# A hybrid decoder layer: the scan's decay by select and biased exponentials, the gated norm's scale at the output projection, q/k roots in batches of four

## The chip, the cores and the metric

The kernel runs on one core of a Trainium2 chip. The metric is the device time of one execution in microseconds (us); lower is better. Engines are named as in the profile: PE (TensorE, matmuls), PEld (its weight loads), DVE (VectorE), ACT (ScalarE), POOL (GpSimd), SP (the queue that issues the DMAs).

## What is computed

One layer of a decoder over 2048 tokens of width 1024, float32. One input projection feeds three branches, whose outputs are joined (512 + 1024 + 512 columns) and mapped back by one output projection:

```python
u = rms_norm(h, norm_g)
q, k, v, z_att, f_raw, z_ssd, xbc, dt_raw, x_lru, z_lru = split(u @ w_in)
y_att = fox_attention(rms_norm(q), rms_norm(k), v, log_sigmoid(f_raw + b)) * silu(z_att)
y_ssd = ssd_mixer(xbc, dt_raw, z_ssd, ...)      # 16 heads x 64, 2 groups, state 128, chunks of 128
y_lru = rglru_mixer(x_lru, ...) * silu(z_lru)
out = h + concat(y_att, y_ssd, y_lru) @ w_out
```

Inside `ssd_mixer`, for each chunk of 128 tokens and each of the 2 groups of 8 heads:

```python
seg  = a_cs[l] - a_cs[s]                  # running sums of the log decay, per head
lmat = exp(where(l >= s, seg, -inf))      # decay, 0 above the diagonal
y    = (C B^T * lmat) @ (x dt)  +  (C @ state) * exp(a_cs)  +  x * d_skip
state = state * exp(total) + B^T @ (x dt * exp(a_cs[-1] - a_cs))
gated = rms_norm(y * silu(z), over the group's 512 columns) * norm_g
```

## The kernel before

**Precision.** A float32 matrix product is made of float32r matmuls: each operand is split into a high part (a cast) and a low part (operand minus high part), and three products are summed in PSUM. So a product over 1024 channels is 8 x 3 matmuls of 128 rows.

**Stages.** (1) x is loaded, normalised, transposed and split (L195-292). (2) `weights` (L172) brings groups of 256 columns of `w_in` to SBUF, eight tiles each, ACT casting the high part (L186) and DVE or POOL making the low part (L187); the tiles turn over in a pool of `NSL` = 11 high and 11 low slots (L161). There are 22 such groups. First come the columns of x, B, C with convolution and silu (L379-413), then the first v/z group, then the linear recurrent branch (L484-576), then z of the state-space branch (L579-591), with `gates` (L416) ahead of its second group. (3) The scan: `ssd_unit` (L608) for 16 chunks x 2 groups, and written after it the projections of q, k, v and z in four column groups (L737-766, `group_vz` L328). On the chip these two run interleaved. (4) Attention (L787-895): per head and 256 queries, scores, exponentials, transposes of the probabilities, product with v. Between its steps a filler is fed in: the first sweep of the output projection (L929-976), over the rows of `w_out` that need no attention (state-space group 1 and the recurrent branch). (5) The second sweep, over state-space group 0 and attention.

**Order.** Each engine runs its queue in order. The program is written in the order above; the Tile framework orders each engine's queue when the program is built and inserts the semaphores. `fill` (L987) advances the filler by 256 ticks over 288 steps of attention; one tick is the three matmuls of one row tile of `w_out`.

**The scan's unit.** Five loads from DRAM (x, z, B, B and C transposed). PE makes the scores `cb` (L623), DVE masks them with `tri` into `cbm` (L625). Per half of the heads (4 heads), the running sums are loaded as rows to all partitions (`ab`, L637), POOL subtracts the column's own sum (L638), DVE clamps to at most 0 (L640), ACT takes the exponential of 512 columns at once (L641), POOL multiplies by `cbm` (L642), and PE multiplies each head's tile with x dt (L645). DVE adds the skip term (L649) and the part from the carried state (L652-656), and multiplies by the gate (L657). ACT squares and sums (L661), DVE takes the inverse root in twelve small instructions (L662, `rsqrt` L110, three Newton steps), ACT scales y (L664). For the next state, ACT and POOL split B and the scaled x (L599), and PE makes three float32r products into `pn` (L604-606). The state is decayed by POOL and added by DVE (L680-682). `store` transposes y and writes it to DRAM. The five PSUM tiles of a unit (`cb`, `py`, `po`, `pn`, `pty`) share a pool of three banks.

**q and k.** For each of 8 pairs of token tiles: projection (`proj_tok2`), copy and squares by ACT, sums by DVE (L748), `rsqrt` on 8 columns, scaling (L753), four transposes, then high and low parts (L762-764) and stores. The tile `qk` has two buffers, and `group_vz` takes its `vs` tile from the same ones.

**Output projection.** Per token tile and 512 output columns, 8 row tiles x 3 matmuls sum into one PSUM bank (L971-973); DVE adds the residual (L974). `parts` names the two kinds of four row tiles. The first sweep has one PSUM bank, the second five.

Of the kernel before, what the change touches and what calls it, by code (L numbers as in the profile page):

```python
# [8 lines left out]
F32 = mybir.dt.float32  # L9
F32R = mybir.dt.float32r  # L10
# [3 lines left out]
ALU = mybir.AluOpType  # L14
# [4 lines left out]
P = 128  # L19
# [8 lines left out]
NSL = 11  # L28
# [14 lines left out]
def hybrid_block(ctx, tc, x, norm_g, w_in, q_norm_g, k_norm_g, forget_b, ssd_conv_w, ssd_conv_b,  # L43
# [45 lines left out]
    tri = ctile("tri", [P, P])          # 1 where column >= partition  # L89
# [12 lines left out]
    acs = ctile("acs", [P, NT, 16])  # L102
    eacs = ctile("eacs", [P, NT, 16])
    dec = ctile("dec", [P, NT, 16])
    etot = ctile("etot", [P, NT, 16])
    lsp = ctile("lsp", [P, 4])
    nlsp = ctile("nlsp", [P, 4])

    # y = v ** -0.5 by Newton's method from a first guess on the bits of v
# [10 lines left out]
    # y = -(v * scale + EPS) ** -0.5 of one column: a root, then one of Newton's steps  # L120
# [9 lines left out]
    # y = log(1 + exp(xin))  # L130
# [23 lines left out]
    # ======================= input projection =======================  # L154
# [7 lines left out]
    # the two parts of u, transposed: [512 tokens][channel tile]  # L162
# [9 lines left out]
    def weights(cols, rawp=wrp, eng=V):  # L172
        """cols: list of (first column, width). Returns the two parts of the float32 weights."""
# [20 lines left out]
    with tpool(name="p0", bufs=2) as p0, tpool(name="p01", bufs=1) as p01, \  # L194
# [71 lines left out]
        for tb in range(4):  # L266
# [12 lines left out]
            if tb == 0:  # L279
# [4 lines left out]
                # halve what goes into silu(y) = (1 + tanh(y / 2)) * (y / 2); 1/8 of the logits; signs  # L284
# [43 lines left out]
    def group_vz(pool, p):  # L328
# [4 lines left out]
        for t2 in range(8):  # L333
            vs = pool.tile([P, 2, 2, P], F32R, name=f"vs{p}_{t2}", tag="qk")
# [80 lines left out]
    rtx.close()  # L415
    def gates(g1):  # L416
# [20 lines left out]
        acs2 = acs.rearrange("p a b -> p (a b)")  # L437
# [42 lines left out]
    group_vz(g0, 0)  # L480
    g0x.close()

# [115 lines left out]
    # the two parts of a tile  # L598
    def split(src, h, l):  # L599
        A.copy(h, src)  # L600
        G.tensor_tensor(l, src, h.bitcast(F32), op=ALU.subtract)

    def mm3(ps, st, mv):
        T.matmul(ps, st[0], mv[0], start=True, stop=False)  # L604
        T.matmul(ps, st[0], mv[1], start=False, stop=False)
        T.matmul(ps, st[1], mv[0], start=False, stop=True)

    def ssd_unit(c, g):  # L608
# [15 lines left out]
        cbm = s1.tile([P, P], F32, name=f"cbm{u}", tag="cbm")  # L624
        V.tensor_tensor(cbm, pc[:, 0:P], tri, op=ALU.mult)  # L625
# [7 lines left out]
        for q in range(2):  # L633
# [4 lines left out]
            G.tensor_tensor(ab, ab, acs[:, c, qs].unsqueeze(2).broadcast_to([P, 4, P]),  # L638
                            op=ALU.subtract)
            V.tensor_scalar(ab, ab, 0.0, None, op0=ALU.min)  # L640
            A.activation(ab, ab, AF.Exp)  # L641
            G.tensor_tensor(ab, ab, cbm.unsqueeze(1).broadcast_to([P, 4, P]), op=ALU.mult)  # L642
# [16 lines left out]
        ss = s2.tile([P, 1], F32, name=f"ss{u}", tag="ss")  # L659
        rs = s2.tile([P, 1], F32, name=f"rs{u}", tag="rs")  # L660
# [76 lines left out]
    with tpool(name="ap", bufs=2) as pool, tpool(name="ap1", bufs=1) as ap1:  # L737
        for p in range(4):
# [28 lines left out]
            if p > 0:  # L767
                group_vz(pool, p)
# [269 lines left out]
```

## Time and profile before

| | |
|---|---|
| runs of the kernel | 2180.85, 2184.38, 2186.16 us; median 2184.38 |
| span of the profiled execution | 2186.6 us, 2.2 us above that median |
| mean granted TensorE clock | 0.973 of full |

The profile's own execution is timed by its span. "Busy" is the time in which an engine ran instructions; PE's matmuls overlap, so the mean length of one is longer than the step from one to the next. "Idle before ... <- X" is the time that an engine stood before instructions of a group, and what ended it. A group's line gives line of code, engine, operation, output <- inputs, shapes, count | busy us, mean ns of one | idle before it.

### The profile page before, as it was taken

The numbers are of one execution on the slowest core, as the hardware profiler recorded it, in microseconds if no ns is written. First come the engines' busy times: TensorE is split into PE (matmuls) and PEld (weight loads), VectorE is DVE, ScalarE is ACT, GpSimd is POOL, SyncE is SP. The second block draws the span as 40 slices with busy tenths as digits, with TensorE's granted clock in tenths as the row PEclk, the third lists the DMA queues.
The fourth block names the chain that finished last, engine by engine and source line by source line (L and its number), as shares of the span: only waits on it lengthen the run. The fifth ranks groups of instructions, "written<-read, shape, count | busy, mean of one in ns | idle before, by whom it ended". The sixth has DMA issues, their size and how long they took to land. (4 is left out here: it accounts for less than half of the span.)

```text
span 2186.6 us, 36465 instructions
## 1 busy us (share of the span) xinstructions
PE 2038.9 (93%) x12515; PEld 1795.1 (82%) x12515; DVE 1439.2 (66%) x3342; ACT 958.2 (44%) x1885; POOL 697.2 (32%) x874
## 2 busy tenths in 40 slices
PE   7999999999999997888878889899999999998999
PEld 6788889877799987777778778788888888887887
DVE  6655563688772179986998795667777777775211
ACT  7444442566621133332334332555565556554110
POOL 0000011555400046656666651133332323222110
PEclk9999999999999999899899999899999999999999
DMA  5122243111123244454445546753554355224443
GB/s 192 49 58 68 76 114 104 30 40 40 39 82 94 69 119 138 132 155 127 127 121 169 142 122 176 210 141 105 145 151 118 103 144 152 76 67 149 155 136 110
DMA packets 277818, 248.44 MB, mean 114 GB/s; under 512 B 58724, under 2 KB 225152, under 8 KB 275584
## 3 DMA queue, kind: packets, MB, share of 16 engines
q1 hardware_dynamic: 277472, 246.07, 39.0%
q8 instruction: 99, 1.62, 0.3%
q14 instruction: 87, 0.71, 0.1%
q0 software_dynamic: 160, 0.03, 0.1%
HBM read 159.83 MB, written 86.18 MB: 113 GB/s over the span
## 5 line engine op out<-in xcount | busy, mean ns | idle before, releaser
L874 ACT CAST ph<-T 128x512 fp32r<-128x512 f32 (+2 forms) x352 | 162.8, 489 | 159.9 <-PE T L867 115.1
L875 DVE TENSOR_TENSOR pl<-T,ph 128x512 fp32r<-128x512 f32 (+2 forms) x352 | 191.3, 565 | 60.6 <-ACT ph L874 57.2
L971 PE MATMUL po<-woh,mh 128*128 128x512 f32 x512 | 214.6, 419 | 1.9 <-ACT mh L954 1.2
L973 PE MATMUL po<-woh,ml 128*128 128x512 f32 x512 | 201.5, 395 | 0.0
L972 PE MATMUL po<-wol,mh 128*128 128x512 f32 x512 | 200.3, 391 | 0.0
L867 PE MATMUL T<-ident,L 128*128 128x128 f32 x1088 | 171.7, 278 | 9.0 <-ACT L L818 7.5
L818 ACT ACTIVATE L<-L,mx 128x1920 f32<-128x1920 f32 (+15 forms) x128 | 154.5, 1207 | 57.1 <-DVE mx L817 53.4
L373 DVE SCALAR_TENSOR_TENSOR accx<-rtx,cv,accx 128x512 f32<-128x512 f32 x144 | 104.5, 753 | 87.1 <-ACT accx L370 77.1
L322 PE MATMUL pxx<-uh,wh 128*128 128x512 f32 x384 | 153.2, 402 | 4.5 <-ACT rtx L365 3.3
L853 PE MATMUL O<-ph,vv 128*128 128x256 f32 x576 | 153.2, 287 | 2.7 <-ACT ph L874 2.6
L323 PE MATMUL pxx<-ul,wh 128*128 128x512 f32 x384 | 154.0, 402 | 0.0
L314 PE MATMUL pqk<-wh,ul 128*128 128x256 f32 x512 | 153.5, 300 | 0.0
L313 PE MATMUL pqk<-wl,uh 128*128 128x256 f32 x512 | 152.6, 298 | 0.5 <-DVE wl L187 0.5
L312 PE MATMUL pqk<-wh,uh 128*128 128x256 f32 x512 | 152.4, 298 | 0.5 <-ACT wh L186 0.5
L324 PE MATMUL pxx<-uh,wl 128*128 128x512 f32 x384 | 152.6, 399 | 0.0
L854 PE MATMUL O<-pl,vv 128*128 128x256 f32 x576 | 150.9, 288 | 0.4 <-DVE pl L875 0.3
L313 PE MATMUL pzs<-wl,uh 128*128 128x256 f32 x512 | 145.5, 285 | 3.0 <-POOL wl L187 3.0
L312 PE MATMUL pzs<-wh,uh 128*128 128x256 f32 x512 | 145.4, 285 | 0.5 <-ACT wh L186 0.5
L314 PE MATMUL pzs<-wh,ul 128*128 128x256 f32 x512 | 144.4, 283 | 0.0
L867 PEld LDWEIGHTS T<-ident,L 128*128 128x128 f32 x1088 | 127.9, 142 | 19.9 <-ACT L L818 12.0
L807 POOL TENSOR_SCALAR_AFFINE_SELECT cm<-cb 128x384 f32<-128x384 f32 (+3 forms) x128 | 58.8, 460 | 256.6 <-DVE mx L814 210.4
L812 PE MATMUL S<-kh,qh 128*128 128x512 f32 (+2 forms) x320 | 129.3, 405 | 10.7 <-DVE mx L814 7.4
(321 smaller groups left out, 5983.5 us busy)
## 6 DMA issues: line engine op xcount, KB each, us to landing
ab<-acs_d SPq DMA_DIRECT2D x64, 256.0 KB
wr<-in_w_in_dram SPq DMA_DIRECT2D x192, 64.0 KB
wr<-in_w_in_dram SPq DMA_DIRECT2D x80, 128.0 KB
xt<-in_x_dram SPq DMA_DIRECT2D x16, 512.0 KB
xs_d<-stx SPq DMA_DIRECT2D x32, 256.0 KB
v_d<-vs SPq DMA_DIRECT2D x32, 256.0 KB
zs_d<-zs SPq DMA_DIRECT2D x32, 256.0 KB
xs<-xs_d SPq DMA_DIRECT2D x32, 256.0 KB
```

Source lines behind the costliest of these rows:

```text
L312: T.matmul(ps[:, i, :], h[k][:, sl], wh[k], start=(k == 0), stop=False)
L313: T.matmul(ps[:, i, :], h[k][:, sl], wl[k], start=False, stop=False)
L314: T.matmul(ps[:, i, :], l[k][:, sl], wh[k], start=False, stop=(k == KD - 1))
L322: T.matmul(ps, wh[k][:, ms], uh[tb][k], start=(k == 0), stop=False)
L323: T.matmul(ps, wh[k][:, ms], ul[tb][k], start=False, stop=False)
L818: A.activation(lt[:, 0:n], lt[:, 0:n], AF.Exp, bias=mx, accum_out=sm[:, i:i + 1])
L867: ins = T.transpose(pt[:, jj, i * P:(i + 1) * P], L[i][:, kt * P:(kt + 1) * P], ident)
L874: A.copy(ph[:, ja, ca], pt[:, ja, ca])
L875: V.tensor_tensor(pl[:, ja, ca], pt[:, ja, ca], ph[:, ja, ca].bitcast(F32), op=ALU.subtract)
L971: T.matmul(ps, mh[:, j, :], h[:, cs], start=(j == 0), stop=False)
L972: T.matmul(ps, mh[:, j, :], l[:, cs], start=False, stop=False)
L973: T.matmul(ps, ml[:, j, :], h[:, cs], start=False, stop=(j == 7))
```

## The change

Seven edits. `NSL` goes from 11 to 9. In the scan: POOL selects the loaded rows (NEG where the row's token is earlier than the column's), ACT takes four exponentials of 128 columns, each with the head's negated sum as bias, and DVE multiplies with the scores straight from PSUM; the subtraction, the clamp and the masked scores go. The gated norm's sum of squares is kept in `rsn`, the inverse roots of all 32 units are taken at once after the scan, and y is stored unscaled. The next state's product is one float32 matmul without a split. In the output projection, where the scale is now applied, the pieces are 256 columns wide: the two kinds of rows sum into two halves of one bank, and DVE evicts each half by itself, one of them with the scale; the filler advances 512 ticks over the 288 steps. The q/k roots are taken for four pairs of token tiles at once (`NQ` = 4), with five buffers (`QB` = 5) for `qk` and `vs`. The tables `nacs`, `eacs`, `dec` stand in a pool that ends with the scan.

```diff
-NSL = 11
+NSL = 9
+NQ = 4
+QB = 5
...
+    nacs, eacs, dec = (sg.tile([P, NT, 16], F32, name=nm) for nm in ("nacs", "eacs", "dec"))
...
+        V.tensor_scalar(nacs.rearrange("p a b -> p (a b)"), pa[:, 0:256], -1.0, None,
+                        op0=ALU.mult)
...
-        V.tensor_tensor(cbm, pc[:, 0:P], tri, op=ALU.mult)
...
-            G.tensor_tensor(ab, ab, acs[:, c, qs].unsqueeze(2).broadcast_to([P, 4, P]),
-                            op=ALU.subtract)
-            V.tensor_scalar(ab, ab, 0.0, None, op0=ALU.min)
-            A.activation(ab, ab, AF.Exp)
-            G.tensor_tensor(ab, ab, cbm.unsqueeze(1).broadcast_to([P, 4, P]), op=ALU.mult)
+            G.affine_select(out=ab, in_=ab, pattern=[[0, 4], [1, P]], compare_op=ALU.is_ge,
+                            fill=NEG, base=0, channel_multiplier=-1)
+            for e in range(4):
+                i = g * 8 + q * 4 + e
+                A.activation(ab[:, e, :], ab[:, e, :], AF.Exp, bias=nacs[:, c, i:i + 1])
+            V.tensor_tensor(ab, ab, pc[:, 0:P].unsqueeze(1).broadcast_to([P, 4, P]),
+                            op=ALU.mult)
...
-        A.activation(sq, y2, AF.Square, accum_out=ss)
-        V.tensor_scalar(ss, ss, 1.0 / 512.0, 4.0 * EPS, op0=ALU.mult, op1=ALU.add)
-        rsqrt(s2, rs, ss, 1, f"rg{u}")
-        A.activation(y2, y2, AF.Copy, scale=rs)
+        A.activation(sq, y2, AF.Square, accum_out=rsn[:, c, g:g + 1])
...
-            split(bm, bh, bl)
...
-            split(x2, xh, xl)
-            mm3(pn, (bh, bl), (xh, xl))
+            T.matmul(pn, bm, xe.rearrange("p h d -> p (h d)"), start=True, stop=True)
...
+    V.tensor_scalar(rs2, rs2, 1.0 / 512.0, 4.0 * EPS, op0=ALU.mult, op1=ALU.add)
+    V.tensor_copy(rsv, rs2)
+    rsqrt(s2, rs2, rsv, NT * 2, "rg")
...
+            for th in range(8 // NQ):
...
+                for i in range(NQ):
...
+                    V.tensor_reduce(ss[:, i, :], sq.rearrange("p i (h d) -> p (i h) d", d=64),
+                                    axis=AX.X, op=ALU.add)
...
+                rsqrt(ap1, r2_, s2_, NQ * 8, f"rk{p}{th}")
+                for i, qk in enumerate(qks):
...
-            for n in range(2):
-                cs = slice(n * 512, n * 512 + 512)
+            for n in range(4):
+                cs = slice(n * 256, n * 256 + 256)
...
-                ps = psP.tile([P, 512], F32, name=f"po{t}_{n}_{ks[0]}", tag="P")
+                ps = psP.tile([P, 2, 256], F32, name=f"po{t}_{n}_{ks[0]}", tag="P")
...
-                    T.matmul(ps, mh[:, j, :], h[:, cs], start=(j == 0), stop=False)
+                    o = ps[:, j // 4, :]
+                    T.matmul(o, mh[:, j, :], h[:, cs], start=(j == 0), stop=False,
+                             skip_group_check=True)
...
-                V.tensor_tensor(xr, xr, ps, op=ALU.add)
+                for j, (kind, _) in enumerate(parts):
+                    if kind in (0, 1):
+                        V.scalar_tensor_tensor(xc, ps[:, j, :], rsn[:, t, kind:kind + 1], xc,
+                                               op0=ALU.mult, op1=ALU.add)
+                    else:
+                        V.tensor_tensor(xc, xc, ps[:, j, :], op=ALU.add)
...
-        want = count[0] * 256 // 288
-        if want > count[1]:
-            count[1] = want
+        want = count[0] * 512 // 288
+        while want > count[1]:
+            count[1] += 1
```

More of the change, by code (lines that the diff above doesn't have):

```diff
@@ L333, in group_vz @@
         for t2 in range(8):
-            vs = pool.tile([P, 2, 2, P], F32R, name=f"vs{p}_{t2}", tag="qk")
+            vs = vpool.tile([P, 2, 2, P], F32R, name=f"vs{p}_{t2}", tag="qk")
             zt = pool.tile([P, 2, P], F32, name=f"zt{p}_{t2}", tag="zt")
@@ L436, in gates @@
         V.tensor_tensor(adt, dt, alg.unsqueeze(1).broadcast_to([P, NT, 16]), op=ALU.mult)
-        acs2 = acs.rearrange("p a b -> p (a b)")
+        acs2 = g1.tile([P, 256], F32, name="acs")
         pa = psY.tile([P, 512], F32, name="pacs", tag="Y")
@@ L735, in load_q @@
         heads[h][3:] = [qh, ql]
[L737 removed]
+    with tpool(name="ap", bufs=2) as pool, tpool(name="ap1", bufs=1) as ap1, \
+            tpool(name="qkp", bufs=QB) as qkp:
         for p in range(4):
             w = weights([(C_Q + p * P, P), (C_K + p * P, P)])
[L740 to L766 removed]
@@ new lines, in hybrid_block @@
+            for th in range(8 // NQ):
+                ss = pool.tile([P, NQ, 8], F32, name=f"sqk{p}_{th}", tag="sqk")
+                rs = pool.tile([P, NQ, 8], F32, name=f"rqk{p}_{th}", tag="rqk")
+                qks = []
+                for i in range(NQ):
+                    t2 = th * NQ + i
+                    qk = qkp.tile([P, 2, 256], F32, name=f"qk{p}_{t2}", tag="qk")
+                    qks.append(qk)
+                    ps = proj_tok2(w, t2, f"pqk{p}_{t2}")
+                    A.copy(qk, ps)
+                    sq = ap1.tile([P, 2, 256], F32, name=f"sq{p}_{t2}", tag="sqq")
+                    A.activation(sq, ps, AF.Square)
+                    V.tensor_reduce(ss[:, i, :], sq.rearrange("p i (h d) -> p (i h) d", d=64),
+                                    axis=AX.X, op=ALU.add)
+                s2_, r2_ = (z.rearrange("p a b -> p (a b)") for z in (ss, rs))
+                V.tensor_scalar(s2_, s2_, 1.0 / 64.0, EPS, op0=ALU.mult, op1=ALU.add)
+                rsqrt(ap1, r2_, s2_, NQ * 8, f"rk{p}{th}")
+                for i, qk in enumerate(qks):
+                    t2 = th * NQ + i
+                    qv = qk.rearrange("p i (h d) -> p (i h) d", d=64)
+                    V.tensor_tensor(qv, qv, rs[:, i, :].unsqueeze(2).broadcast_to([P, 8, 64]),
+                                    op=ALU.mult)
+                    pt = pst.tile([P, 2, 256], F32, name=f"ptq{p}_{t2}", tag="pt")
+                    for j in range(2):
+                        for i2 in range(2):
+                            T.transpose(pt[:, j, i2 * P:(i2 + 1) * P],
+                                        qk[:, i2, j * P:(j + 1) * P], ident)
+                    ts = slice(t2 * 256, (t2 + 1) * 256)
+                    for j, (wn, gn) in enumerate((("q", "qg"), ("k", "kg"))):
+                        sh = pool.tile([P, 256], F32R, name=f"sth{p}_{t2}_{j}", tag="sth")
+                        sl = pool.tile([P, 256], F32R, name=f"stl{p}_{t2}_{j}", tag="stl")
+                        A.activation(sh, pt[:, j, :], AF.Copy, scale=c1(gn))
+                        V.scalar_tensor_tensor(sl, pt[:, j, :], c1(gn), sh.bitcast(F32),
+                                               op0=ALU.mult, op1=ALU.subtract)
+                        dma(qk_d[wn, "h", p][:, ts], sh.bitcast(F32))
+                        dma(qk_d[wn, "l", p][:, ts], sl.bitcast(F32))
@@ L767, in hybrid_block @@
             if p > 0:
-                group_vz(pool, p)
+                group_vz(pool, qkp, p)
             if p == 2:
```

70 lines of the change are left out of this document (18 added, 52 removed).

## The prediction

> **What bounds the kernel now.** I read the page's shares first, then the busy time of each engine by stage, then what PE waits for inside the worst stage, then the groups of instructions.
>
> ```profile
> span 2186.6 us, 36465 instructions
> ...
> PE 2038.9 (93%) x12515; PEld 1795.1 (82%) x12515; DVE 1439.2 (66%) x3342; ACT 958.2 (44%) x1885; POOL 697.2 (32%) x874
> ...
> PE   7999999999999997888878889899999999998999
> ...
> DVE  6655563688772179986998795667777777775211
> ```
>
> PE is busy 93% of the span, but the slices say that it is not everywhere the limit: about slices 14 to 24 PE stands at 8 tenths or less while DVE stands at 9. That is where the scan of the state-space branch and the q, k, v projections run together. The busy time by stretches (PE, PEld, DVE, ACT, POOL, then the granted clock) gives the size:
>
> ```profile
> 601.30:765.30 164.00, 164.00 (x1382) 163.90 (x1381) 62.30 (x146) 32.48 (x65) 9.73 (x12) 1.00 0.27 81
> 765.30:1366.60 601.30, 504.24 (x3616) 466.50 (x3616) 499.35 (x1241) 214.13 (x475) 338.18 (x308) 0.93 0.49 139
> 1421.30:1967.90 546.60, 538.06 (x3488) 477.27 (x3487) 406.42 (x1165) 318.68 (x640) 163.25 (x319) 1.00 0.44 120
> ```
>
> The first row is pure projection: PE without a gap at full clock. The third is attention with the first output sweep: PE 98%. The middle one is the scan stage: 601.3 us, PE busy 504.2, so 97.1 us idle, and the granted clock is 0.93, so about 601.3 x 0.07 = 42 us of the rest is lost to half-rate time. At full clock the same PE work is 504.2 x 0.93 = 469 us. DVE is busy 499 us there, 83%. What PE waited for inside this stage (total us, times, longest):
>
> ```profile
> PE ptq L757 <- DVE qk L753: 30.3, 15, 5.8
> PE py L645 <- POOL ab L642: 18.8, 16, 1.9
> PE pn L605 <- POOL xel L601: 14.9, 11, 3.0
> PE pty L689 <- DVE yo L654: 7.8, 7, 2.4
> PE pn L604 <- ACT bh L600: 7.6, 8, 1.8
> ```
>
> Five rows carry 79.4 of the 97.1 us, and each waits at the end of a chain over DVE, POOL or ACT which the change cuts. How the gaps reach the clock shows at two of them (start, length, the idle time ahead in brackets) and the 2 us stretch that follows:
>
> ```profile
> 918.73 1.10 PE L645 MATMUL py<-xd,ab 128*128 128x64 f32 x8 [1.76 <-POOL ab L642]
> 923.37 0.66 PE L757 MATMUL ptq<-ident,qk 128*128 128x128 f32 x4 [2.62 <-DVE qk L753]
> 924.00:926.00 2.00, 2.00 (x14) 2.00 (x12) 1.86 (x10) 0.62 (x1) 0.21 (x1) 0.57 0.04 8
> ```
>
> Gaps of 1.76 and 2.62 us, 2 us of work between them, and from 924 matmuls run at clock 0.57.
>
> **The change, part by part.** DVE in the scan stage first: the groups that go or shrink, and the price of what comes.
>
> ```profile
> L640 DVE TENSOR_SCALAR ab<-ab 128x512 f32<-128x512 f32 x64 | 58.9, 921 | 40.1 <-POOL ab L638 40.1
> L118 DVE SCALAR_TENSOR_TENSOR rs<-rg_t,rs 128x1 f32<-128x1 f32 x96 | 32.6, 340 | 1.1
> L117 DVE SCALAR_TENSOR_TENSOR rg_t<-rg_t,rs 128x1 f32<-128x1 f32 x96 | 29.8, 311 | 1.1
> L116 DVE TENSOR_TENSOR rg_t<-rs,ss 128x1 f32<-128x1 f32 x96 | 28.8, 300 | 1.3
> L118 DVE SCALAR_TENSOR_TENSOR rqk<-rk_t,rqk 128x8 f32<-128x8 f32 x96 | 33.3, 347 | 1.4
> L117 DVE SCALAR_TENSOR_TENSOR rk_t<-rk_t,rqk 128x8 f32<-128x8 f32 x96 | 31.6, 329 | 1.4
> L116 DVE TENSOR_TENSOR rk_t<-rqk,sqk 128x8 f32<-128x8 f32 x96 | 32.3, 336 | 1.4
> L649 DVE TENSOR_TENSOR y<-py,xs 128x512 f32<-128x512 f32 x32 | 21.8, 682 | 0.8 <-PE py L645 0.7
> ```
>
> Gone: the clamp, 64 x 0.921 = 58.9 us; the Newton steps of the gated norm, 32.6 + 29.8 + 28.8 = 91.2 us (one root over 32 columns at the end takes their place, nine such steps of some 0.34 us, 3 us in all, beside projections). The q/k roots run 8 times instead of 32: three quarters of 33.3 + 31.6 + 32.3 = 97.2 are 72.9 us. Wider rows (32 columns instead of 8) should cost little: a step on 1 column takes 340 ns and on 8 columns 347. Added: 64 products of the decay with the score tile in PSUM; the nearest row is L649, the same shape with one operand in PSUM, 682 ns, so 43.6 us. The net is 223 - 44 = -179 us (I leave out the three small steps ahead of each root and the masked product, which also go). DVE falls from 499 to about 320 us in a stage that I expect to last over 500: it is no longer near the limit.
>
> The other engines of the same chain (shapes kept apart where one line has several):
>
> ```profile
> L638 POOL TENSOR_TENSOR ab<-ab,acs 128x512 f32<-128x512 f32 x64 | 74.0, 1157 | 107.2 <-DMA ab<-acs_d 102.9 <-DMA ct<-ct_d 4.3
> L642 POOL TENSOR_TENSOR ab<-ab,cbm 128x512 f32<-128x512 f32 x64 | 82.1, 1290 | 146.4 <-DVE cbm L625 123.4 <-ACT ab L641 7.4 <-ACT xeh L600 3.7
> L641 ACT ACTIVATE ab<-ab 128x512 f32<-128x512 f32 x62 | 39.1, 631 | 114.9 <-DVE ab L640 114.7
> L600 ACT CAST bh<-bm 128x128 fp32r<-128x128 f32 x30 | 8.7, 289 | 11.5 <-POOL ab L642 11.5
> L807 POOL TENSOR_SCALAR_AFFINE_SELECT cm<-cb 128x512 f32<-128x512 f32 x32 | 19.6, 614 | 52.2 <-DVE mx L814 48.7 <-DMA xr<-in_x_dram 3.0
> ```
>
> POOL loses 74.0 + 82.1 us, and the splits besides, and gains 64 selects at 0.614 = 39 us: from 338 to about 220 us or less. ACT replaces 64 exponentials of 512 columns by 256 of 128. No exponential of that shape stands in the trace; between 0.158 us (a quarter of 631 ns) and 0.289 us (the 128x128 cast) I take the second, 74 us against 40.4, since the small row carries an instruction's fixed part. The row scale and the two casts that go pay for most of that. ACT was at 214 of 601 us and has room. The chain of one half unit was 1.157 + 0.921 + 0.631 + 1.290 = 4.0 us after its load lands; it becomes 0.614 + 4 x 0.289 + 0.682 = 2.45 us. The score bank is now held until the second product instead of the mask. Five PSUM tiles per unit take turns over three banks, so the state product takes the bank that the scores had; its matmuls stand behind the unit's own decay products on PE anyway, and I cost that at nothing (a late product would cost what L645 waits now).
>
> The state product: three passes of 512 columns become one fp32 product, whose price is that of the carried state's product, beside the step of the 512-column matmuls in the last sweep:
>
> ```profile
> 904.69 1.08 PE L652 MATMUL po<-st,ct 128*128 128x512 f32 x2
> 905.73 0.28 PE L313 MATMUL pqk<-wl,uh 128*128 128x256 f32 x1
> 2104.18 0.39 PE L971 MATMUL po<-woh,mh 128*128 128x512 f32 x1
> 2106.92 0.39 PE L971 MATMUL po<-woh,mh 128*128 128x512 f32 x1
> ```
>
> From 904.69 to 905.73 the fp32 pair holds PE 1.04 us. From 2104.18 to 2106.92 twelve matmuls of 512 columns go by, 0.228 us each; three are 0.685. So 30 x 0.35 = +10 us on PE at most; one interrupted trio in the old order pays a tenth more, so I take +8. The stage's floor is 469 + 8 = 477 us.
>
> What idle time stays: ptq 30.3 to 10 (8 chains instead of 32), py 18.8 to 8 (the chain is 2.45 instead of 4.0 us), pn 22.5 to 2 (the splits are gone, only the scaled x is awaited), pty 7.8 to 3 (no root ahead of it), the remaining 17.7 to 5: 28 us. Half-rate loss in proportion, 42 x 28 / 97 = 12 us. The stage comes to 477 + 28 + 12 = 517 us, that is **-84 us**.
>
> The rows at 918.73 to 924.00 above show gaps of 1.76 and 2.62 us that ended in half rate. The Trainium skill (TensorE: Matmul & The Clock Gate, Part 1: The HAM clock gate) has the clock fall only after an idle window of about 3.4 us; by that the short waits that I leave would cost no clock and the sum would be 12 us lower.
>
> The output projection now needs each product in two halves of 256 columns, so 1536 matmuls of 512 become 3072 of 256. The stretch 601.30:765.30 holds 1382 matmuls of 256 columns in 164.0 us, 0.1187 us each, weight load included: two are 0.2374 against 0.228. That is 1536 x 0.009 = **+14 us**, half in attention, half in the last sweep; PE has next to no gap in attention (third row above) and steps without a pause in the last sweep, so all of it is on the path. The Trainium skill (TensorE: Matmul & The Clock Gate, Back-to-back issue gap) gives, for isolated matmuls, N / 2.4 GHz plus 2.5 ns; by that a pair of halves costs 2.5 ns more and the sum would be 10 us lower.
>
> ```profile
> L971 PE MATMUL po<-woh,mh 128*128 128x512 f32 x512 | 214.6, 419 | 1.9 <-ACT mh L954 1.2
> L972 PEld LDWEIGHTS po<-wol,mh 128*128 128x128 f32 x512 | 96.8, 189 | 14.7
> L974 DVE TENSOR_TENSOR xr<-xr,po 128x512 f32<-128x512 f32 x64 | 43.8, 684 | 125.7 <-PE po L973 122.4 <-DMA xr<-pt_d 3.2
> L875 DVE TENSOR_TENSOR pl<-T,ph 128x256 fp32r<-128x256 f32 x64 | 26.7, 418 | 5.0 <-ACT ph L874 4.3
> L313 PE MATMUL pzs<-wl,uh 128*128 128x256 f32 x512 | 145.5, 285 | 3.0 <-POOL wl L187 3.0
> ```
>
> Evictions: 64 of 0.684 us become 256 of about 0.418, 107 us of DVE instead of 44. In attention DVE goes from 406 to about 440 of 547 us, still beside PE. The first sweep has one PSUM bank, handed over 64 times instead of 32; so far L971 waited 1.9 us in all. I take **+4 us**; ends 0 and the rival below.
>
> Weight slots, 11 to 9: two tiles fewer are ready when a group of columns starts. Where POOL makes the low part, PE already waits 3.0 us (last row); where DVE does, hardly. Of the six POOL groups three to five at 1 to 2 us each, clock included: **+6 us**; ends 0 and the rival. Gates gain one small copy, tables move to another pool: nothing, the projections cover it. q/k order: a batch of four needs its tiles kept, five are there; PE has the next projections to do meanwhile.
>
> **Sum.** -84 + 14 + 4 + 6 = -60 us: 2186.6 becomes 2126.6. The profiled span is 2.2 us above the median of the runs, so I forecast **2124 us**.
>
> **The rivals.**
> *Half of the idle stays.* Each queue's order is fixed beforehand; a batch's root, DVE behind it and the decay chain may simply make fewer, longer waits. For: ptq waits up to 5.8 us at a time even now. Against: PE is 98% busy in attention with DVE at 74%. Idle 48 and clock 21: 546 us, -55 + 24 = -31, 2153 us.
> *PE never runs dry.* Idle 5, clock 2: 484 us, -117 + 24 = -93, 2091 us. The rule of the Trainium skill (TensorE: Matmul & The Clock Gate, Part 1) that short waits leave the clock alone leans this way.
> *Weight slots bite.* At each of 22 group starts 2 us of wait plus 1 us of half rate, 66 us in place of 6: 2184 us, no change. Against: L313 above, 3.0 us in all with two POOL groups.
> *The one bank of the first sweep (slower).* After the last matmul of a piece, PE's next piece waits for DVE's queue (one 0.69 us instruction) and two evictions of 0.418, with the drain some 1.8 us. If PE stands for each, 64 x 1.8 = 115 us: +51, 2235 us. It decides from about 1 us a handover. Against: 1.9 us now over 32 handovers.
> *Weight loads set the step.* A load takes 189 ns busy (L972); were it not overlapped, 3072 x 0.189 = 581 against 351 us, +230 and 2340 us. Against: the 0.1187 us a step measured above. The Trainium skill (TensorE: Matmul & The Clock Gate, Back-to-back issue gap) also makes narrow matmuls dear, with sustained figures of 131 ns at 512 columns and 81 at 128; this trace's steps don't agree.
> *The stage is not set by these waits* but by the scan's own order: no gain, +24, 2208 us.
>
> **How the numbers follow.** Forecast 0.60, half idle 0.17, never dry 0.10, slots 0.05, one bank 0.05, weight loads 0.01, scan order 0.02. A change under 0.3% (6.5 us) can't be told from none. Faster: the first three and a part of the slots, 0.89; same 0.03; slower 0.08. The range takes in never dry and half idle with the cost terms' ends: 2085 to 2160.
>
> **What would show it.** Right: the scan stage some 80 us shorter with PE over 90% and clock near 0.98; DVE about 320 us there; no pn wait; ptq waits around 10 us; 3072 output matmuls stepping 0.119 us; the last sweep some 7 us longer. Wrong: PE still under 88% in the scan stage with waits on ptq or py; L971's successors waiting on DVE evictions in attention; waits on wl at group starts over 20 us.

## The result and the profile after

| | before | after |
|---|---|---|
| median of four runs each on the same chip | 2183.95 us (2180.85 to 2186.16) | 2092.44 us (2082.31 to 2094.80) |
| ratio after / before, 95% interval | | 0.9565 (0.9546 to 0.9584) |
| span of the profiled execution | 2186.6 us | 2092.4 us (its time 2094.4) |

The change saves 91.5 us, where 60 were forecast. The top of the page of the kernel after, which answers to the first lines that the prediction shows:

```profile
span 2092.4 us, 38943 instructions
...
PE 2011.2 (96%) x14021; PEld 1838.4 (88%) x14021; DVE 1278.1 (61%) x2844; ACT 954.3 (46%) x1985; POOL 542.0 (26%) x750
...
PE   7999999999999999998999998999999999998999
...
DVE  6654555488874226767576245677787787774333
```

In the slices the valley of PE is gone, and so is DVE's ridge beside it. To see where the time went I cut both traces at the same three events: the end of the last `pzs` matmul (the scan stage begins), the end of the last `pvz` matmul (all projections are done) and the last `pf` matmul of attention. Columns: stretch, length, busy time of PE, PEld, DVE, ACT and POOL, granted clock, DMA share, GB/s. Before:

```profile
773.10:1381.50 608.40, 511.33 (x3676) 473.60 (x3675) 499.47 (x1242) 213.60 (x474) 338.18 (x308) 0.94 0.49 139
1381.50:2006.90 625.40, 603.70 (x3810) 529.05 (x3810) 463.69 (x1311) 370.88 (x740) 184.22 (x351) 0.98 0.47 131
2006.90:2186.60 179.70, 175.18 (x796) 143.34 (x794) 33.48 (x49) 17.97 (x30) 18.75 (x15) 1.00 0.42 132
```

After:

```profile
773.60:1275.50 501.90, 477.83 (x3643) 440.80 (x3643) 289.87 (x553) 207.82 (x571) 175.27 (x183) 0.99 0.58 169
1275.50:1893.40 617.90, 596.15 (x4540) 558.82 (x4538) 478.92 (x1406) 372.41 (x738) 184.02 (x349) 0.98 0.47 131
1893.40:2092.40 199.00, 190.30 (x1600) 190.09 (x1600) 70.12 (x147) 17.90 (x32) 21.95 (x18) 0.97 0.41 126
```

The start is as long as before (773.6 against 773.1 us). The scan stage falls from 608.4 to 501.9 us, **-106.5**. Attention and the last sweep together go from 805.1 to 816.9 us, **+11.8** (the first sweep of the output projection fills attention, so its border moves and only the sum is compared). 0.5 - 106.5 + 11.8 = -94.2 us, the difference of the spans.

The stage can be cut further. Its length is PE's idle time, PE's busy time reduced to full clock, and what half rate adds to it (half of the time that PE was busy in stretches of clock 0.5). Before: 97.1 + 475.5 + 35.8. After: 24.1 + 471.4 + 6.4. What PE still waits for inside the stage (total us, times, longest):

```profile
PE py L642 <- DVE ab L638: 6.5, 11, 1.3
PE pty L674 <- DVE yo L651: 3.3, 2, 2.9
PE pqk L312 <- ACT wh L186: 3.0, 3, 2.4
PE po L649 <- ACT yt L676: 2.6, 1, 2.6
PE cb L619 <- DVE y L646: 2.2, 3, 1.4
PE ptq L758 <- DVE qk L753: 1.4, 1, 1.4
```

The long rows of before, `ptq` with 30.3 us and `pn` with 22.5, have shrunk to 1.4 and to nothing. The groups of the new decay chain and of the batched root:

```profile
L637 ACT ACTIVATE ab<-ab,nacs 128x128 f32<-128x128 f32 x248 | 80.1, 391 | 130.0 <-POOL ab L633 122.2 <-PE cb L619 7.4
L633 POOL TENSOR_SCALAR_AFFINE_SELECT ab<-ab 128x512 f32<-128x512 f32 x62 | 44.0, 710 | 108.0 <-DMA ab<-acs_d 54.8 <-DMA ct<-ct_d 18.9 <-DVE y L646 10.0
L638 DVE TENSOR_TENSOR ab<-ab,cb 128x512 f32<-128x512 f32 x62 | 42.1, 683 | 56.2 <-ACT ab L637 39.6 <-POOL xs L645 8.3 <-DMA gt_d<-yt 2.6
L117 DVE SCALAR_TENSOR_TENSOR rk_t<-rk_t,rqk 128x32 f32<-128x32 f32 x24 | 6.6, 273 | 0.7
```

An exponential takes 391 ns by itself and, since neighbours overlap, 80.1 / 248 = 0.323 us in its row of four, not 0.289; the chain is 0.710 + 4 x 0.323 + 0.683 = 2.69 us, where the prediction had 2.45 and before had 4.0.

### The profile page after: what moved, and what is told of

It reads as the page before. It is cut to its first block, busy times and chain, and to the rows that moved or that the text cites. A ratio compares the mean times of both kernels' runs of the same rounds, so it can differ in the third digit from the quotient of the medians.

```text
span 2092.4 us, 38943 instructions
## 1 busy us (share of the span) xinstructions
PE 2011.2 (96%) x14021; PEld 1838.4 (88%) x14021; DVE 1278.1 (61%) x2844; ACT 954.3 (46%) x1985; POOL 542.0 (26%) x750
## 5 line engine op out<-in xcount | busy, mean ns | idle before, releaser
L977 PE MATMUL po<-woh,mh 128*128 128x256 f32 x1024 | 295.2, 289 | 7.3 <-ACT mh L956 7.3
L981 PE MATMUL po<-woh,ml 128*128 128x256 f32 x1024 | 289.3, 283 | 0.0
L979 PE MATMUL po<-wol,mh 128*128 128x256 f32 x1024 | 288.2, 282 | 0.0
L977 PEld LDWEIGHTS po<-woh,mh 128*128 128x128 f32 x1024 | 193.8, 189 | 10.4 <-ACT mh L956 8.0
L979 PEld LDWEIGHTS po<-wol,mh 128*128 128x128 f32 x1024 | 194.4, 190 | 2.7
L981 PEld LDWEIGHTS po<-woh,ml 128*128 128x128 f32 x1024 | 193.4, 189 | 1.0
L312 PE MATMUL pqk<-wh,uh 128*128 128x256 f32 x512 | 147.8, 293 | 3.0 <-ACT wh L186 3.0
```

What stands on the lines that cost most here:

```text
L977: T.matmul(o, mh[:, j, :], h[:, cs], start=(j == 0), stop=False, skip_group_check=True)
L979: T.matmul(o, mh[:, j, :], l[:, cs], start=False, stop=False, skip_group_check=True)
L981: T.matmul(o, ml[:, j, :], h[:, cs], start=False, stop=(j % 4 == 3), skip_group_check=True)
```

## The experiments

The theory: the scan sets its own pace, unit after unit, through a chain of POOL, ACT and DVE instructions (decay first, then state, then norm), and PE stands where the projections woven into it do not cover that chain. The rival: DVE was simply too full (499 of 608 us), so any edit that relieves DVE helps in proportion, the batched q/k roots as much as the decay. The table holds every run; the rows of stage and scan come from each kernel's own trace, cut as above (scan: first to last `py` matmul).

| kernel | median us | ratio to before (95%) | scan | stage | idle | busy at half rate | attention and last sweep |
|---|---|---|---|---|---|---|---|
| before | | 1 | 540.4 | 608.4 | 97.1 | 71.6 | 805.1 |
| after | 2092.44 | 0.9565 (0.9546 to 0.9584) | 356.8 | 501.9 | 24.1 | 12.7 | 817.0 |
| u_decay | 2271.55 | 1.0393 (1.0362 to 1.0424) | 356.3 | 689.0 | 134.2 | 165.3 | 807.7 |
| u_state | 2237.85 | 1.0230 (1.0202 to 1.0259) | 319.8 | 650.8 | 102.5 | 142.5 | 812.3 |
| u_norm | 2089.31 | 0.9559 (0.9541 to 0.9576) | 369.0 | 511.4 | 29.6 | 19.8 | 799.9 |
| u_qk | 2079.26 | 0.9513 (0.9495 to 0.9532) | 347.7 | 497.7 | 22.2 | 6.8 | 808.3 |
| pad64 | 2184.81 | 1.0008 (0.9993 to 1.0022) | 264.8 | 596.0 | 76.9 | 89.0 | 809.1 |
| q1 | 2091.05 | 0.9580 (0.9564 to 0.9596) | 356.0 | 505.7 | 27.9 | 10.1 | 809.2 |
| q1_d | 2129.43 | 0.9753 (0.9734 to 0.9773) | 438.6 | 539.8 | 49.4 | 33.2 | 808.3 |
| q1_s10 | 2113.09 | 0.9680 (0.9664 to 0.9696) | 389.2 | 516.4 | 39.3 | 12.0 | 814.6 |
| dec_only | 2112.18 | 0.9677 (0.9655 to 0.9699) | 405.7 | 534.0 | 55.2 | 12.2 | 803.5 |
| st_only | 2164.25 | 0.9917 (0.9899 to 0.9935) | 488.1 | 588.8 | 83.8 | 60.4 | 801.8 |
| norm_only | 2152.02 | 0.9860 (0.9833 to 0.9887) | 496.2 | 564.7 | 70.1 | 42.2 | 806.1 |
| best | 2091.83 | 0.9584 (0.9563 to 0.9606) | 349.7 | 499.9 | 24.0 | 6.8 | 816.8 |

Kernel before on the same chip: 2186.05 us for the u_ kernels, 2184.70 for pad64 and the q1 kernels, 2182.67 for the last four.

### One part taken out of the change at a time

**u_decay**: the old decay, all else as changed.

```diff
+        cbm = s1.tile([P, P], F32, name=f"cbm{u}", tag="cbm")
+        V.tensor_tensor(cbm, pc[:, 0:P], tri, op=ALU.mult)
...
-            G.affine_select(out=ab, in_=ab, pattern=[[0, 4], [1, P]], compare_op=ALU.is_ge,
-                            fill=NEG, base=0, channel_multiplier=-1)
-            for e in range(4):
-                i = g * 8 + q * 4 + e
-                A.activation(ab[:, e, :], ab[:, e, :], AF.Exp, bias=nacs[:, c, i:i + 1])
-            V.tensor_tensor(ab, ab, pc[:, 0:P].unsqueeze(1).broadcast_to([P, 4, P]),
-                            op=ALU.mult)
+            G.tensor_tensor(ab, ab, nacs[:, c, qs].unsqueeze(2).broadcast_to([P, 4, P]),
+                            op=ALU.add)
+            V.tensor_scalar(ab, ab, 0.0, None, op0=ALU.min)
+            A.activation(ab, ab, AF.Exp)
+            G.tensor_tensor(ab, ab, cbm.unsqueeze(1).broadcast_to([P, 4, P]), op=ALU.mult)
```

> The changed kernel with the decay done the old way: running sums subtracted on POOL, clamped on DVE, one exponential of 512 columns, product with masked scores on POOL. Theory A (chains: PE waited at the ends of chains over DVE, POOL and ACT, and each cut removes its own waits): DVE gets only some 25 us back, but the chain to py is 4.0 us again; waits of py of 12 to 19 us and a few us of half rate return, 12 to 25 us slower than the changed kernel, 2105 to 2117. Rival B (DVE load: the stage follows the DVE time, half a microsecond per microsecond): +13 us, 2105. Rival C (one part carries it, the q/k batches): under 5 us.

Measured: 2271.55 us, slower than the kernel before although three of four parts are still in. Its largest wait of PE in the stage:

```profile
PE py L642 <- POOL ab L639: 124.5, 35, 9.1
```

**u_state**: the old state product, three passes over split operands.

```diff
-            T.matmul(pn, bm, xe.rearrange("p h d -> p (h d)"), start=True, stop=True)
+            bh = s1.tile([P, P], F32R, name=f"bh{u}", tag="cbm")
+            bl = s2.tile([P, P], F32R, name=f"bl{u}", tag="bt")
+            split(bm, bh, bl)
+            xh = s1.tile([P, 512], F32R, name=f"xeh{u}", tag="xeh")
+            x2 = xe.rearrange("p h d -> p (h d)")
+            xl = s1.tile([P, 512], F32R, name=f"xel{u}", tag="xd")
+            split(x2, xh, xl)
+            mm3(pn, (bh, bl), (xh, xl))
```

> The changed kernel with the state product split into three float32r products again. Theory A: POOL gets 51 us and ACT 27 us back, pn waits for the splits again, 10 to 15 us with the clock, and PE saves some 7 us of work: 0 to 10 us slower than the changed kernel, 2092 to 2102. Rival B (DVE load alone): no wait returns, 7 us faster, 2085. Rival C: the same, within 7 us.

Measured: 2237.85 us, slower than before as well:

```profile
PE py L651 <- POOL xd L630: 70.8, 29, 3.8
PE pn L610 <- POOL xel L606: 19.3, 19, 2.4
```

Neither result can be read as the price of its part. In both traces the scan has lost its cover: the first `ptq` matmul of the q/k projections stands at 1160.7 us (u_decay) and 1123.2 us (u_state), after the last `py` at 1139.0 and 1100.7, where in the kernel after it comes at 819.9, early in the scan. Both kernels add a tile to the scan's memory (512 bytes a partition; 2.5 KB). pad64, below, tests whether that alone does it.

**u_norm**: root and scale inside the unit again, and with them 512-column pieces and one eviction each in the output projection.

```diff
-        A.activation(sq, y2, AF.Square, accum_out=rsn[:, c, g:g + 1])
+        A.activation(sq, y2, AF.Square, accum_out=ss)
+        V.tensor_scalar(ss, ss, 1.0 / 512.0, 4.0 * EPS, op0=ALU.mult, op1=ALU.add)
+        rsqrt(s2, rs, ss, 1, f"rg{u}")
+        A.activation(y2, y2, AF.Copy, scale=rs)
...
-                ps = psP.tile([P, 2, 256], F32, name=f"po{t}_{n}_{ks[0]}", tag="P")
+                ps = psP.tile([P, 512], F32, name=f"po{t}_{n}_{ks[0]}", tag="P")
...
-        want = count[0] * 512 // 288
+        want = count[0] * 256 // 288
```

> The changed kernel with the norm's root and the scaling of y inside the scan unit, and the output projection in pieces of 512 columns with one eviction, as before the change. Theory A: in the scan stage 15 to 30 us come back (DVE gets 100 us back, pty and ptq wait behind roots), in the output projection 8 to 14 us are saved: 2 to 20 us slower than the changed kernel, 2094 to 2112. Rival B: +50 - 11, some 39 us slower, 2131. Rival C: 11 us faster, 2081.

Measured: 2089.31 us, no difference from after. Its two stretches, the stage and all behind it:

```profile
773.50:1284.90 511.40, 481.80 (x3644) 444.28 (x3643) 358.95 (x924) 229.23 (x602) 178.40 (x183) 0.98 0.58 166
1284.90:2084.80 799.90, 775.73 (x4604) 669.44 (x4603) 496.38 (x1360) 388.65 (x770) 203.89 (x366) 0.99 0.46 132
```

The moved scale is worth 9.5 us in the stage (511.4 to 501.9) and costs 17 behind it (799.9 to 817.0), of which 7 go with a slower matmul step in the trace of after that most kernels with the same lines do not have (see the output projection below). With the other parts in, it brings nothing.

**u_qk**: one token pair to a root.

```diff
-NQ = 4
+NQ = 1
```

> The changed kernel with batches of one token pair (32 roots of 8 columns again), buffers unchanged. Theory A: waits of ptq come back, but with the rest of DVE's load gone they are shorter than before, 20 to 35 us slower than the changed kernel with the clock, 2112 to 2127. Rival B: DVE gets about 88 us back, +44, 2136. Rival C: nearly the whole gain is lost, +80 or more, 2170 or above.

Measured: 2079.26 us, 13 us faster than after by the medians (0.9513 against 0.9565, the intervals do not touch). The stage's row and the `ptq` wait:

```profile
773.10:1270.80 497.70, 475.47 (x3643) 437.98 (x3643) 344.45 (x841) 207.13 (x571) 176.37 (x183) 0.99 0.59 170
```

```profile
PE ptq L758 <- DVE qk L753: 1.6, 1, 1.6
```

DVE has 55 us more to do (344 against 290) and the stage is 4 us shorter. So at this load, 290 to 344 of some 500 us, DVE is not what PE stands for, and an edit that relieves it further brings nothing. What set the stage when DVE had 499 of 608 us to do, this run does not say. The short `ptq` wait is there without any batching.

### A pad of 256 bytes

**pad64**: the change, and one tile that nothing reads.

```diff
+    pad = s1.tile([P, 64], F32, name="pad")
+    G.memset(pad, 0.0)
```

> The changed kernel with one unused tile of 256 bytes per partition added to the scan's pool; no other edit. Theory M (memory: the q/k pools lie behind the scan's in the same memory, and once they overlap by a few bytes, the q/k projections wait until the scan has ended; this, and not the old decay or the split as such, made the two undone kernels slower than the kernel before): the scan runs alone, PE has no filling work, q/k scaling starts only after the scan, 2200 to 2260 us. Theory A (the undone decay and the splits were slow by their own chains): a tile that nobody uses costs nothing, 2092.

Measured: 2184.81 us, the whole gain lost. The stage in two parts, cut at the end of the scan:

```profile
773.70:1045.60 271.90, 199.03 (x959) 139.25 (x959) 158.39 (x218) 117.34 (x345) 171.24 (x181) 0.83 0.60 175
1045.60:1369.60 324.00, 319.93 (x2686) 319.20 (x2685) 130.64 (x335) 99.74 (x225) 1.08 (x2) 0.99 0.38 115
```

First the scan almost alone (18 of the 199 us in which PE is busy are q/k projections), 272 us at clock 0.83; then, from the first `ptq` at 1067.9 us on, projections alone. The pools of the q/k projections are opened where the program has closed the scan's pools, and lie next to them. As long as the two do not overlap they run woven together. In the program of after, the buffers of `qk` end at byte 195872 of each partition and the scan's lowest tile begins at 195936, 64 bytes on; in pad64 it begins at 195680, in u_decay at 195424 and in u_state at 193376. There the two overlap, and the q/k tiles wait for the scan's end. That is worth 92 us, as much as the whole change. It also gives u_decay and u_state their meaning: against pad64, which has the same loss of cover, they are 87 and 53 us slower, and the bare scan takes 356.3 and 319.8 us instead of 264.8. So the scan's own pace hangs on both chains, on the decay most. In none of these three bare scans is an engine full: DVE is busy 54 to 59% of the scan, PE 63 to 72%, POOL 65% in pad64, 80% in u_decay and 71% in u_state. This speaks for chains from engine to engine, and against the load of any one of them.

### Parts taken out with the memory held clear

**q1** leaves the q/k batch out with its payment in weight slots; **q1_d** has the old decay besides, **q1_s10** the old state product (with one slot fewer, to pay for its tiles).

```diff
-NSL = 9
-NQ = 4
-QB = 5
+NSL = 11
+NQ = 1
+QB = 2
```

q1_d adds the lines of u_decay to these, q1_s10 those of u_state, with

```diff
-NSL = 11
+NSL = 10
```

> The changed kernel with the q/k part as before: batches of one pair, two buffers for qk and vs, eleven weight slots. So the change without its q/k part and without what paid for its memory. Theory A2 (the scan's decay, norm and state edits carry the whole gain; waiting for four pairs costs PE more than the roots' DVE time saves): 2070 to 2085. Theory B (DVE load): 2125 or more, since 88 us of DVE come back.

> The kernel q1 with the decay done the old way (subtraction and masked product on POOL, clamp, exponential of 512 columns). Here it fits beside the q/k pools. Theory A2: 30 to 70 us slower than q1, since POOL gets 113 us and the decay chain its 4.0 us back; waits of py on ab return. Theory M alone: within 10 us of q1.

> The kernel q1 with the state product split in three again, and ten weight slots, so that it fits. Theory A2: pn waits for the splits again, 5 to 25 us slower than q1. Theory M alone: within 5 us of q1, or faster by 7, the matmul time saved.

Measured: q1 2091.05 us, the same as after: batch and slots together bring nothing. q1_d 2129.43, so the decay is worth 38 us on top of the other parts; q1_s10 2113.09, 22 us slower than q1. Of these only the 11 in the stage can be put down to the state product: by the spans of the profiled runs, 3 lie ahead of the stage, where this kernel has one weight slot less, and 5 behind it, where its trace has the slower matmul step too. The waits of q1_d in its stage:

```profile
PE ptq L758 <- DVE qk L753: 12.6, 13, 2.1
PE py L642 <- POOL ab L639: 11.9, 14, 2.2
```

From q1 to q1_d nothing of the q/k code changes, only the decay, and the `ptq` wait is back (12.6 us; q1 has 2.5). With the old state product it is back too (13.0 in q1_s10). So these waits belong to the scan. How POOL gets into the q/k roots shows at the longest `ptq` wait of the kernel before (start, length, idle time ahead in brackets):

```profile
1071.85 0.17 DVE L116 TENSOR_TENSOR rk_t<-rqk,sqk 128x8 f32<-128x8 f32 x1
1072.05 0.98 DVE L117 SCALAR_TENSOR_TENSOR rk_t<-rk_t,rqk 128x8 f32<-128x8 f32 x1
...
1071.97 1.04 POOL L638 TENSOR_TENSOR ab<-ab,acs 128x512 f32<-128x512 f32 x1 [1.99 <-DMA ct<-ct_d]
...
1076.21 1.12 PE L757 MATMUL ptq<-ident,qk 128*128 128x128 f32 x4 [5.78 <-DVE qk L753]
```

The first Newton step on 8 columns takes 0.17 us, the next, beside a POOL instruction, 0.98. Of the 288 such steps in that stage, 196 have no POOL instruction beside them and take 164 ns on average, 170 at most; the other 92 take 0.71 us on average, up to 1.27. So the 347 ns of the prediction's row are a mixture, and some 95 of the 188 us of the two roots' steps are this stretching (the 576 steps at their medians, 166 and 158 ns, would be 93). Steps of over 0.6 us and the `ptq` wait in the kernels with one pair a root: before 60 and 30.3 us, norm_only 61 and 32.8, st_only 36 and 18.8, q1_s10 47 and 13.0, q1_d 43 and 12.6, dec_only 32 and 10.7, q1 32 and 2.5, u_qk 31 and 1.6. The waits come down roughly with the stretched steps, not exactly, so this is part of the reason and not shown to be all of it.

### Parts added alone to the kernel before

Each has the change's placement of the small tables and its q/k loop at one token pair a root; norm_only has 10 slots.

dec_only:

```diff
-            G.tensor_tensor(ab, ab, acs[:, c, qs].unsqueeze(2).broadcast_to([P, 4, P]),
-                            op=ALU.subtract)
-            V.tensor_scalar(ab, ab, 0.0, None, op0=ALU.min)
-            A.activation(ab, ab, AF.Exp)
-            G.tensor_tensor(ab, ab, cbm.unsqueeze(1).broadcast_to([P, 4, P]), op=ALU.mult)
+            G.affine_select(out=ab, in_=ab, pattern=[[0, 4], [1, P]], compare_op=ALU.is_ge,
+                            fill=NEG, base=0, channel_multiplier=-1)
+            for e in range(4):
+                i = g * 8 + q * 4 + e
+                A.activation(ab[:, e, :], ab[:, e, :], AF.Exp, bias=nacs[:, c, i:i + 1])
+            V.tensor_tensor(ab, ab, pc[:, 0:P].unsqueeze(1).broadcast_to([P, 4, P]),
+                            op=ALU.mult)
```

> The kernel before with the decay edit alone (select, biased exponentials, product from PSUM), slots, buffers, norm, state product and output projection as before. Theory A2 (the scan's chains over POOL, ACT and DVE set its pace, and the decay is the largest): 40 to 70 us faster than before, 2115 to 2145. Theory B (DVE load): 12 us faster. If the edits only work together, under 20 us.

st_only:

```diff
-            mm3(pn, (bh, bl), (xh, xl))
+            T.matmul(pn, bm, xe.rearrange("p h d -> p (h d)"), start=True, stop=True)
```

> The kernel before with the single float32 state product alone. Theory A2: the waits of pn on the splits go, 22 us in the profile of before, and POOL loses 51 us: 15 to 35 us faster, 2150 to 2170. Theory B: no gain, or 7 us slower by the matmul's price.

norm_only, with the pieces of 256 columns of the output projection:

```diff
-        A.activation(sq, y2, AF.Square, accum_out=ss)
-        V.tensor_scalar(ss, ss, 1.0 / 512.0, 4.0 * EPS, op0=ALU.mult, op1=ALU.add)
-        rsqrt(s2, rs, ss, 1, f"rg{u}")
-        A.activation(y2, y2, AF.Copy, scale=rs)
+        A.activation(sq, y2, AF.Square, accum_out=rsn[:, c, g:g + 1])
...
+                        V.scalar_tensor_tensor(xc, ps[:, j, :], rsn[:, t, kind:kind + 1], xc,
+                                               op0=ALU.mult, op1=ALU.add)
```

> The kernel before with the norm edit alone: root after the scan, scale at the eviction, pieces of 256 columns; ten weight slots. Theory A2: the scan stage gains 10 to 30 us by 105 us less DVE, the output projection costs 10 to 17: between 20 us faster and 7 slower, 2165 to 2192. Theory B: 50 - 12, 38 us faster, 2146.

Measured: the decay alone -70.5 us, the norm alone -30.7, the state product alone -18.4; 120 together, more than the 91.5 of the whole. The same wait in dec_only, st_only and norm_only, in this order:

```profile
PE ptq L773 <- DVE qk L768: 10.7, 10, 2.0
```

```profile
PE ptq L757 <- DVE qk L752: 18.8, 13, 2.8
```

```profile
PE ptq L774 <- DVE qk L769: 32.8, 19, 4.8
```

None of them batches, yet the decay alone takes `ptq` from 30.3 to 10.7 us. The norm alone gained more than the theory had for it (2152, where it gave 2165 to 2192 and the rival 2146). Counted as DVE's time in the trace, the rival does well on this side: the stage falls by 74 us in dec_only, 44 in norm_only and 20 in st_only, and DVE's busy time in it by 81, 58 and 22 (from 499.5 to 418.6, 441.6 and 478.0), the stretched steps included. At the other end it fails: from q1 to q1_d DVE gets 55 us more and the stage 34, from after to u_qk DVE gets the same 55 and the stage loses 4. What sets the two apart is the decay's chain and POOL's time in the stage, 113 us more in q1_d and 1 in u_qk. For the stage of the kernel before, the length of the chain, POOL's time and DVE's time fall together with the decay edit, and no run here parts them. The overlap of the gains has a plain reason: the stage's work at full clock is 471 to 477 us in every kernel of the table, idle and half-rate time are all there is to win, and after the decay only some 60 us of them are left.

### A version with both

**best** is u_qk with the scale applied to the rows of the gated product ahead of the output projection (POOL multiplies them by the scales, stored once and loaded broadcast), so that the 512-column pieces with one eviction stay (NSL 9 and QB 5 as in the change).

```diff
+                    rb = o1.tile([P, P], F32, name=f"rb{t}_{k0}", tag="rb")
+                    dma(rb, rs_d[t * 2 + kind:t * 2 + kind + 1, :].partition_broadcast(P))
+                    G.tensor_tensor(mt, mt, rb.unsqueeze(1).broadcast_to([P, 4, P]), op=ALU.mult)
...
-                ps = psP.tile([P, 2, 256], F32, name=f"po{t}_{n}_{ks[0]}", tag="P")
+                ps = psP.tile([P, 512], F32, name=f"po{t}_{n}_{ks[0]}", tag="P")
```

> The changed kernel with batches of one pair, and the norm's scale put on when the first operand of the output projection is loaded: the 32 x 128 inverse roots go to DRAM, each token tile's row is loaded to all partitions, POOL multiplies the loaded tile by it, and the pieces are 512 columns with one eviction again. If the 256-column pieces cost what the trace of the changed kernel shows, 11 to 17 us less than with them: 2063 to 2080. If the row's load or POOL's product comes late for the next tile's cast, waits before the output matmuls, 2085 or more.

Measured: 2091.83 us, no gain. The stage is nearly as short as u_qk's (499.9), and PE's work behind it is as small (767.8 us at full clock, 768.4 in u_qk), but attention and last sweep together take 816.8 us instead of 808.3: 5 us more of idle time and 4 of half rate. The largest waits behind the stage:

```profile
PE S L820 <- DVE mx L822: 9.5, 17, 1.6
PE T L875 <- ACT L L826: 8.4, 13, 1.3
```

The first output sweep is the filler of attention; its weave with the scores seems to have come out worse in this version, for a reason that I did not separate. The fastest kernel measured stays u_qk.

## Why the prediction was right, and where its steps were not

**Place and direction: right.** The scan stage carries all of the gain, the output projection gives a little back.

**The stage, -84 forecast, -106.5 measured.** By its three terms: idle -69 forecast, -73.0 measured; half rate -23 (12 left of the 35 that the forecast's sum leaves for it beside 469 and 97; its text has 42, the trace of before 35.8), -29.4; work at full clock +8, -4.1. The mis-sized term is the last, the fp32 state product, which missed by 12 of the 22 us. Work did not grow with it: the kernels that differ by it, and otherwise by a weight slot or the place of the small tables, have 471.1 (split, q1_s10) against 472.8 us (q1), and 475.5 (split, before) against 474.8 (st_only), so within 2 us nothing, not +8. (u_state, with 477.0 against 471.4, has the split dearer still.) Both prices of the term were off. The float32 product holds PE 0.91 us in the kernel after, not 1.04:

```profile
782.37 1.08 PE L659 MATMUL pn<-xe,bm 128*128 128x512 f32 x2
783.28 0.38 PE L619 MATMUL cb<-ct,bt 128*128 128x128 f32 x2
```

And the three old passes never stand together in the trace of before: each of the 30 products has other matmuls between them, and the passes take 0.317, 0.232 and 0.232 us to the next matmul (medians), 0.78 together where the forecast came to 0.75 with its tenth. By these rows the term is 30 x 0.13, some 4 us; why the stage's work fell by 4.1 all the same stays open.

The idle total (28 forecast, 24.1 measured) was met in part by luck. The rows of the scan came as forecast: `py` 8, measured 6.5 in its one large row; `pn` 2 and none; `pty` 3 and 3.3. But `ptq` came to 1.4 instead of 10, and all the remaining waits to 12.9 instead of 5, and these two misses cancel.

**The reason given for `ptq` was wrong.** The prediction gave 20 us of idle time to eight root chains in place of 32. The waits went, to 1.4 us, but u_qk has 1.6 without the batch, and without it q1_d has 12.6 and q1_s10 13.0: the decay and state edits take them away, not the batch. The batch by itself brings nothing that can be measured; u_qk is the faster kernel without it.

**DVE to about 320 us, POOL to 220 or less.** Measured 290 and 175. That DVE's fall was the cause is refuted for its last 55 us by u_qk; for the rest it came together with the shorter chain. (The prediction reads DVE at 9 tenths in PE's valley; the digits there go from 6 to 9, and the 83% that it goes on with is right.)

**Durations.** The 128-column exponential took 391 ns, outside the bracket of 158 to 289. The Trainium skill (ScalarE: Activation LUTs, What ACT_TABLE_LOAD costs) has the price: an activation whose bias is a column takes 280 ns + 0.833 ns a column, so an estimate by that page is 387 ns, and the trace agrees; the casts that I took for my bracket have no such bias. Further, the select 710 ns instead of 614; the product 683 as taken; a Newton step on 32 columns 256 to 273 ns, less than the 340 taken (0.19 us where the scan's POOL instructions are not beside it, as in pad64); the scaled eviction 481 ns instead of 418. ACT paid some 80 us for its exponentials, as its other work fell, and had the room.

**Output projection, +18 forecast, +11.8 measured.** PE's work rose by 7.3 us (768.6 to 775.9), its idle time by 4.3. The step forecast, 0.1187 us, is what the last sweep of the profiled run shows:

```profile
1949.95 0.28 PE L977 MATMUL po<-woh,mh 128*128 128x256 f32 x1
...
1952.78 0.28 PE L977 MATMUL po<-woh,mh 128*128 128x256 f32 x1
```

24 steps of 0.118 us, so two halves cost 7 ns more than one piece of 0.229, and 1536 pairs would be 11 us. But u_qk, on the same lines of code, steps faster:

```profile
1951.50 0.28 PE L977 MATMUL po<-woh,mh 128*128 128x256 f32 x1
...
1952.86 0.28 PE L977 MATMUL po<-woh,mh 128*128 128x256 f32 x1
```

12 steps of 0.113 us. By the rule weighed in the prediction (the Trainium skill, TensorE: Matmul & The Clock Gate, Back-to-back issue gap) a pair costs 2.5 ns more; the runs show 7 ns more in one kernel and 2 less in the other. u_qk, pad64, q1, q1_d, u_decay and norm_only step at 0.113 in the last sweep, after, u_state and q1_s10 at 0.118, all at full clock in the same order of operands. PE's work behind the stage goes with it: 768.1 to 769.3 us at full clock in the first six, 774.5 to 775.9 in the last three, and 767.8 to 768.8 in the kernels with pieces of 512 columns. So halving the pieces cost PE next to no work where the step is 0.113, and the 7.3 us of the kernel after are its slower step in the last sweep (1536 matmuls x 5 ns are 8 us). Why stays open; the 8 us are over half of u_qk's lead, and the 12 us between after's own runs (2082 to 2095) may be of the same kind.

**Weight slots, +6 forecast.** In the stage `wl` cost 0.8 us, and the stretch ahead of it is 0.5 us longer: nothing. q1 with 11 slots is no faster than after or u_qk with nine.

**The rivals.** PE never running dry gave 2091 us, which is what came out, but not for its reason: idle time is 24 us, not 5, and the number is met because work fell instead of rising and the output cost less. The one bank of the first sweep did not decide: idle time behind the stage rose by 4 us, not 115. The scan's own order as the limit is refuted as it was put (no gain), yet holds a truth that the forecast lacked: where the scan runs bare, its pace is that of its chains, with no engine over 80% busy.

**What no step foresaw** is that all of it rests on 256 bytes. The prediction looked at tiles and slots for their waits, not at where pools come to lie.

## What to carry to other kernels

Where an engine stands at 84% and three others are busy beside it, look for the chain that paces it and test the parts both ways, each taken out of the whole and each added alone: the decay is 70 us alone and 38 at the end, the norm 31 and -3, and only the pair of numbers shows that the gains overlap. After an edit that adds or removes a tile, look where the pools that are opened later come to lie, for a weave of two stages can hang on their not touching. A scale that is moved to an eviction, and splits the matmuls ahead of it, need not be free: behind the stage it cost 1 us here (norm_only against before) to 17 (after against u_norm). And the mean length of a small DVE instruction can be a mixture: look whether the long ones stand beside POOL.

## What the chip showed besides

How much idle time of PE costs clock can be read off the kernel after, since it has so few gaps. Between 773 and 1145 us PE is idle for more than 1.4 us at a stretch only three times (start, length, idle time ahead in brackets):

```profile
854.67 0.68 PE L312 MATMUL pqk<-wh,uh 128*128 128x256 f32 x2 [2.35 <-ACT wh L186]
...
967.10 1.75 PE L649 MATMUL po<-st,ct 128*128 128x512 f32 x2 [2.56 <-ACT yt L676]
...
1115.20 1.12 PE L674 MATMUL pty<-ident,y 128*128 128x128 f32 x4 [2.89 <-DVE yo L651]
```

Stretches of clock 0.5 begin at 854.83, 967.47 and 1114.24 us, 3.4, 3.4 and 6.8 us long, and there are no others up to there; the gaps of 1.39 us and less cost none. But it is not the single gap that decides. In attention of the same trace a stretch begins at 1284.91 us, 6.8 us long, with no gap there longer than 1.34. The four starts lie 33, 43 and 50 times 3.413 us apart, and within each of the 14 traces all starts after the first 60 us lie on one such grid. What counts is PE's idle time in the step of the grid that ends there; for the first and the last of the four (columns as in the tables of stretches):

```profile
851.42:854.83 3.41, 1.06 (x9) 0.85 (x8) 0.34 (x2) 1.78 (x6) 2.46 (x3) 1.00 0.79 197
1281.50:1284.91 3.41, 2.00 (x8) 0.84 (x6) 3.24 (x8) 3.03 (x6) 0.85 (x1) 1.00 1.01 405
```

PE was idle for 2.35 and 1.41 of the 3.41 us. Over all traces from 100 us on, each of the 140 steps at full clock with 1.95 us of idle time or more was followed by half rate, and one of the 7586 with less than 1.2 us; in between it went both ways (87 of 216). The Trainium skill (TensorE: Matmul & The Clock Gate, Part 1: The HAM clock gate) asks for an idle window of about 3.4 us; here 2.35 us of idle time was enough, and at times less. By its rule the short waits would have cost no clock; they cost 6.4 us, about halfway to the 12 of the forecast. That half rate fell more than idle time did (to a sixth and to a quarter) fits the same rows: the waits that stayed are mostly too short for it.

Four small exponentials with a bias per head take 1.29 us in their row, twice the 0.631 us of the one of 512 columns. They paid all the same, since with the select they take the place of 1.157 and 1.290 us on POOL and 0.921 on DVE.
